# A streaming log-sum-exp on one core: in tiles 56 to 62 GpSimd folds one head of each half tile after the exp and adds no bias before it; in the prologue VectorE does the copies and one exp replaces three

## Chip, cores, metric

One core of a Trainium2 chip. The metric is the device time of one execution in microseconds. Its median before was 328.29 us (three runs, 328.19 to 328.30). Engines in the profile: PE is the tensor engine (PEld its weight loads), DVE is VectorE, ACT is ScalarE, POOL is GpSimd, SP is the sync engine, which issues the loads. SBUF is the on-chip memory that holds the tiles, PSUM the one that PE writes its sums to. In the views, the granted clock is the share of the full TensorE clock that PE was given, and the DMA share is the mean busy share of the core's 16 DMA engines, which move the data between the device's memory and SBUF.

## The reference

```python
B, S, D, H = 8, 2048, 2048, 8            # x (8, 2048, 2048) f32, bias (8, 256) f32
x_heads = x.reshape(B, S, H, D // H).transpose(0, 2, 1, 3) + bias[None, :, None, :]
x_tiled = np.repeat(x_heads, 2, axis=2)
mx  = x_tiled.max(axis=-1, keepdims=True)
lse = mx.squeeze(-1) + np.log(np.exp(x_tiled - mx).sum(axis=-1))   # (8, 8, 4096)
```

Every row of 2048 numbers is eight heads of 256. For each head: add the head's bias, exp, sum, log; each result is written twice. x is 134.2 MB and is read once.

## The kernel before

x comes in as 64 tiles of 256 rows (2.1 MB, two rows a partition, so tile halves k = 0 and k = 1) through nine buffers. From tile 56 on each half of a tile is loaded and worked on by itself; I call that a unit. There are three ways to deal with a head, and each stage (a range of tiles) deals its eight heads to them:

- "pe" heads: PE puts bias and x into PSUM, ScalarE takes exp and sums in one instruction (a head sum below);
- weighed heads: ScalarE takes exp(x) in place, VectorE multiplies by exp(bias) and sums (or, `fold`, GpSimd multiplies and halves three times to 32 columns, and VectorE adds up the rest in a small reduction);
- "g" heads: GpSimd adds the bias, ScalarE takes exp, VectorE reduces.

```python
BULK      = dict(pe=2, g0=4, late=True,  fold=0)   # heads 0-1 pe, 2-3 weighed in one piece, 4-7 g
MIXED     = dict(pe=1, g0=4, late=False, fold=0)   # head 0 pe, 1-3 weighed one by one, 4-7 g
PROMPT    = dict(pe=2, g0=8, late=False, fold=0)   # heads 0-1 pe, 2-7 weighed one by one
PROMPT_F1 = dict(pe=2, g0=8, late=False, fold=1)   # ... the last of them folded by GpSimd
PROMPT_F2 = dict(pe=2, g0=8, late=False, fold=2)   # ... the last two
STAGES = [(0, (BULK,)), (50, (MIXED,)), (56, (MIXED, MIXED)), (61, (PROMPT, PROMPT)),
          (62, (PROMPT, PROMPT_F1)), (63, (PROMPT_F2, PROMPT))]   # a pair: one mode per tile half

# prologue: bias row spread over the partitions by PE, weights exp(bias)
for i, c in enumerate(range(G0, D, MM)):
    spread(ps[i], c, c + MM)
    nc.scalar.activation(out=b_rep[:, c - G0 : c - G0 + MM], in_=ps[i], func=ACT.Copy)
for c in range(W0, W2, MM):
    w = w_ps[:, c - W0 : c - W0 + MM]
    spread(w, c, c + MM)
    nc.scalar.activation(out=w, in_=w, func=ACT.Exp)
nc.scalar.activation(out=w_sb, in_=b_rep[:, W1 - G0 :], func=ACT.Exp)

# main loop, cut to its order
for t in range(T):
    for k0, k1, c0, c1 in pieces(t):               # tile 63 comes in seven pieces of columns
        ...                                        # PE: add x to the bias in PSUM; GpSimd: g_add
        if c0 == 0 and (t < T - 1 or k0 == 0): flush(for_pool)   # the unit before: g heads, fold's sum
        done = exp_inplace(...)                    # ScalarE: exp of the weighed heads
        if hf < h1: for_pool.append(fold(...))     # GpSimd: fold
        if c0 == 0 and (t < T - 1 or k0 == 0): flush(for_pe)     # the unit before: pe heads
        for k in ...: for h in range(h0, hf): weigh(...)         # VectorE
        ...                                        # a freed buffer: load(t + NBUF)
    ...                                            # log of a finished batch; after batch 6 store()
flush(for_pe); flush(for_pool); finish_last()      # transpose, log, store of batch 7
```

The softmax here doesn't subtract the row's maximum and nothing guards it: scores larger than these inputs give would overflow.

## Time and profile before

| | before |
|---|---|
| time, us | 328.29 |
| span in the profile, us | 326.5 |
| busy: DVE, ACT, POOL, PE, us | 286.4, 278.5, 288.4, 230.7 |
| DMA rate, 50 to 260 us | 428 GB/s at a DMA share of 1.00 |
| x read | 134.2 MB |

The chain that ended last (the profile follows it back from the last instruction, at each step to what released it) closes so in the kernel before (start, duration, what):

```profile
309.90 10.19 DMA xt<-in_x_dram
...
320.12 0.63 ACT xt L257
320.75 0.01 issue
320.76 0.63 ACT xt L257
321.38 1.47 ACT xt L232 x8
```

In this profile the end hangs on the landing of a piece of tile 63 at 320.1, then on ScalarE's last exps and head sums.

### The profile page before, as it was taken

Reading aid. Unit: us, or ns where it says so; the run is one execution under the profiler, and the core shown is the slowest. Engines: PE = TensorE matmul, PEld = TensorE weight load, DVE = VectorE, ACT = ScalarE, POOL = GpSimd, SP = SyncE. Lnnn points to the kernel's source line nnn. Section 1 sums busy time; section 2 is a strip of 40 time slices with the busy share of each in tenths; the row PEclk is TensorE's granted clock in tenths of the full one; section 3 lists DMA queues with packets and bytes.
Section 4 is the critical chain, followed back from the end, with each engine's and each line's share of the span. In section 5 each row is a group of like instructions: output and inputs, shape, how many; then the busy total and the mean of one; then the engine's idle time right before and its main releaser. Section 6 shows DMA issues by size and latency. Waiting matters only on the chain.

```text
span 326.5 us, 1959 instructions
## 1 busy us (share of the span) xinstructions
PE 230.7 (71%) x391; PEld 67.5 (21%) x391; DVE 286.4 (88%) x318; ACT 278.5 (85%) x574; POOL 288.4 (88%) x88
## 2 busy tenths in 40 slices
PE   6798857777677668967798666686667355575791
PEld 2122211212122212312222212212112101222220
DVE  0029999999999999989998999989998999999994
ACT  3279999798889888799889889899888988799995
POOL 7999899979999999999998999999998999999713
PEclk9999698588967985597658778968987655555576
DMA  8999999999999999999999999999999999999993
GB/s 292 432 434 424 433 430 424 432 426 428 430 428 427 430 430 425 428 434 426 423 432 427 422 435 428 426 434 426 426 433 426 428 432 422 417 421 422 422 386 105
DMA packets 11807, 135.41 MB, mean 415 GB/s; under 512 B 1361, under 2 KB 1489, under 8 KB 2833
## 3 DMA queue, kind: packets, MB, share of 16 engines
q1 hardware_dynamic: 11696, 135.27, 98.5%
q8 instruction: 3, 0.05, 0.1%
q14 instruction: 10, 0.08, 0.1%
q0 software_dynamic: 96, 0.00, 0.0%
q10 hardware_dynamic: 2, 0.01, 0.0%
HBM read 134.23 MB, written 1.05 MB: 414 GB/s over the span
## 4 chain that ended last, share of the span: by engine, by line
DMA 69%; DVE 10%; POOL 7%; ACT 7%; PE 6%; issue 0%; SPq 0%
DMA xt<-in_x_dram 67%; DVE R L274 7%; POOL xt L251 6%; ACT xt L257 5%; PE ps L217 4%; DVE xt L267 2%; DMA b<-bparts 2%; ACT xt L232 2%; PE ps L202 1%; DMA brow<-in_bias_dram 0%; POOL brest L165 0%; POOL brest L167 0%; POOL b L170 0%; PE tpair L330 0%; POOL bparts L164 0%
## 5 line engine op out<-in xcount | busy, mean ns | idle before, releaser
L251 POOL TENSOR_TENSOR xt<-xt,b_rep 128x2048 f32<-128x2048 f32 (+1 forms) x66 | 277.5, 4209 | 22.1 <-DMA xt<-in_x_dram 21.9
L217 PE MATMUL ps<-xt,ident 128*128 128x512 f32 (+1 forms) x244 | 175.7, 852 | 78.8 <-DMA xt<-in_x_dram 78.5
L257 ACT ACTIVATE xt<-xt 128x3072 f32<-128x3072 f32 (+3 forms) x91 | 185.7, 2062 | 20.2 <-POOL xt L251 19.3
L274 DVE TENSOR_REDUCE R<-xt 128x12 f32<-128x3072 f32 (+1 forms) x56 | 181.4, 3240 | 2.3 <-ACT xt L257 0.6
L232 ACT ACTIVATE xt<-ps 128x256 f32<-128x256 f32 x234 | 86.8, 394 | 11.2 <-PE ps L217 11.1
L267 DVE TENSOR_TENSOR xt<-xt,w_ps 128x1024 f32<-128x1024 f32 x50 | 60.9, 1218 | 32.7 <-ACT xt L257 32.6
L217 PEld LDWEIGHTS ps<-xt,ident 128*128 128x128 f32 x244 | 55.3, 256 | 152.8 <-DMA xt<-in_x_dram 111.2
L232 ACT ACTIVATION_READ_ACCUMULATOR xt<-ps 128x1 f32 x234 | 51.0, 220 | 0.0
L202 PE MATMUL ps<-b,ones 3*128 3x512 bf16 (+1 forms) x122 | 47.5, 457 | 2.8 <-ACT xt L232 1.6
L285 DVE CUSTOM_DVE_ANT_0 xt<-xt,w_ps 128x256 f32<-128x256 f32 x95 | 34.0, 417 | 0.3 <-ACT xt L257 0.3
L202 PEld LDWEIGHTS <-ones 3*128 3x128 bf16 x122 | 8.0, 97 | 82.1 <-issue 82.1
L274 DVE TENSOR_REDUCE R_last<-xt 128x4 f32<-128x1024 f32 x10 | 12.2, 1218 | 0.0
L301 POOL TENSOR_TENSOR xt<-xt,w_sb 128x256 f32<-128x256 f32 (+1 forms) x2 | 2.1, 1032 | 8.7 <-ACT xt L257 8.5
L340 ACT ACTIVATE res<-tpair 64x512 f32<-64x512 f32 x7 | 4.1, 588 | 3.5 <-PE tpair L330 3.4
L174 PE MATMUL w_ps<-brow,ones 1*128 1x512 f32 x6 | 6.0, 1109 | 1.3 <-ACT w_ps L186 1.3
L330 PE MATMUL tpair<-ident,R 128*64 128x128 f32 x14 | 3.8, 364 | 3.7 <-DVE R L274 3.7
L186 ACT ACTIVATE w_ps<-w_ps 128x512 f32<-128x512 f32 x3 | 1.7, 582 | 5.4 <-PE w_ps L174 5.4
L174 PE MATMUL ps<-brow,ones 1*128 1x512 f32 x4 | 3.7, 1089 | 2.5 <-DMA brow<-in_bias_dram 2.5
L285 DVE DVE_READ_ACCUMULATOR2_ANT R_last<- 128x1 f32 x63 | 5.3, 84 | 0.0
L180 ACT ACTIVATE b_rep<-ps 128x512 f32<-128x512 f32 x2 | 1.2, 597 | 3.6 <-PE ps L174 3.6
L285 DVE DVE_READ_ACCUMULATOR2_ANT R<- 128x1 f32 x36 | 3.0, 85 | 0.0
L351 PE MATMUL tpair<-ident,R_last 128*128 128x128 f32 x1 | 0.5, 477 | 3.6 <-ACT xt L232 3.6
(24 smaller groups left out, 18.0 us busy)
## 6 DMA issues: line engine op xcount, KB each, us to landing
xt<-in_x_dram SPq DMA_DIRECT2D x56, 2048.0 KB, 31.9
xt<-in_x_dram SPq DMA_DIRECT2D x14, 1024.0 KB, 21.0
xt<-in_x_dram SPq DMA_DIRECT2D x5, 256.0 KB, 11.3
out_dram<-res SPq DMA_DIRECT2D x1, 896.0 KB, 8.0
xt<-in_x_dram SPq DMA_DIRECT2D x2, 384.0 KB, 16.5
out_dram<-res_last SPq DMA_DIRECT2D x1, 128.0 KB, 1.7
b<-bparts POOLq DMA_DIRECT2D x3, 1.0 KB, 6.0
brow<-in_bias_dram ACTq DMA_DIRECT2D x1, 8.0 KB
```

Source lines behind the costliest of these rows:

```text
L174: nc.tensor.matmul(dst, lhsT=ones, rhs=brow[:, c0:c1], start=True, stop=True)
L202: nc.tensor.matmul(p, lhsT=ones3, rhs=each_row(b3, 0, n, kb - ka), start=True, stop=False,)
L217: mm = nc.tensor.matmul(p, lhsT=ident, rhs=xts[t % NBUF][:, ka:kb, 0:n], start=False, stop=True,)
L232: act = nc.scalar.activation(out=xts[t % NBUF][:, k, c : c + Dh], in_=p[:, c : c + Dh], func=ACT.Exp, accum_out=sums[:, k, h : h + 1],)
L251: add = nc.gpsimd.tensor_tensor(out=v, in0=v, in1=each_row(b_rep, c - G0, D - c, k1 - k0), op=ALU.add)
L257: return on_x(t, nc.scalar.activation(out=v, in_=v, func=ACT.Exp), [after])
L267: mul = nc.vector.tensor_tensor(out=f, in0=f, in1=each_row(w_ps, h0 * Dh - W0, n, k1 - k0), op=ALU.mult,)
L274: red = nc.vector.tensor_reduce(out=sums[:, k0:k1, h0:H], in_=v.rearrange("p k (h j) -> p k h j", j=Dh), op=ALU.add, axis=mybir.AxisListTy ...
L285: ttr = nc.vector.tensor_tensor_reduce(out=v, in0=v, in1=w, scale=1.0, scalar=0.0, op0=ALU.mult, op1=ALU.add, accum_out=dst,)
L301: done = nc.gpsimd.tensor_tensor(out=v, in0=v, in1=w_sb[:, h0 * Dh - W1 : h1 * Dh - W1], op=ALU.mult)
L330: nc.tensor.transpose(out=tp[0:nr, k], in_=R[b][:, k].rearrange("p h n -> p (h n)"), identity=ident,)
L340: nc.scalar.activation(out=res[:, b], in_=tv, func=ACT.Ln)
```

## The change

Intent: from tile 56 on no head goes through GpSimd's slow bias add ahead of the exp; one head is folded by GpSimd instead, after the exp, and one summed by ScalarE. In the prologue the idle VectorE does the copies, and one exp in place of three breaks ScalarE's and PE's turn-taking.

```diff
+SINGLE_F1 = dict(pe=1, g0=8, late=False, fold=1)
 STAGES = [
     (0, (BULK,)),
     (50, (MIXED,)),
-    (56, (MIXED, MIXED)),
-    (61, (PROMPT, PROMPT)),
-    (62, (PROMPT, PROMPT_F1)),
+    (56, (SINGLE_F1, SINGLE_F1)),
+    (62, (PROMPT_F1, SINGLE_F1)),
     (63, (PROMPT_F2, PROMPT)),
 ]
@@ prologue
-        nc.scalar.activation(
-            out=b_rep[:, c - G0 : c - G0 + MM], in_=ps[i], func=ACT.Copy
-        )
+        nc.vector.tensor_copy(b_rep[:, c - G0 : c - G0 + MM], ps[i])
     for c in range(W0, W2, MM):
-        w = w_ps[:, c - W0 : c - W0 + MM]
-        spread(w, c, c + MM)
-        nc.scalar.activation(out=w, in_=w, func=ACT.Exp)
+        spread(w_ps[:, c - W0 : c - W0 + MM], c, c + MM)
+    nc.scalar.activation(out=w_ps, in_=w_ps, func=ACT.Exp)
```

## The prediction

> **What bounds the kernel now.** I read the page's slices first, then the chain that ended last, the sync engine's waits, the stretches of the last microseconds, and the timeline of ScalarE and VectorE there. From the page of the kernel before (one digit or figure per 8.16 us):
>
> ```profile
> DVE  0029999999999999989998999989998999999994
> DMA  8999999999999999999999999999999999999993
> GB/s 292 432 434 424 433 430 424 432 426 428 430 428 427 430 430 425 428 434 426 423 432 427 422 435 428 426 434 426 426 433 426 428 432 422 417 421 422 422 386 105
> ```
>
> Three compute engines are 85% to 88% busy, which tempts one to look for the gain there. But the DMA row is full from the second slice to the last but one. 134.2 MB of x have to come in; at the 428 GB/s that the stretch from 50 to 260 us shows, that is 134.2 / 0.428 = 313.6 us of the 326.5 us span. The rest is about 2 us before the first bytes, some slow transfer near the end, and the tail after the last landing.
>
> Could the transfers have been late because a buffer came free late? The sync engine's waits (what it waited for, us in total, times, longest):
>
> ```profile
> SPq L135 <- DVE R L274: 230.1, 50, 18.1
> SPq L135 <- DMA xt<-in_x_dram: 51.5, 19, 4.5
> SPq L344 <- DMA xt<-in_x_dram: 2.1, 1, 2.1
> ```
>
> The loads do wait for VectorE's reductions, but the page gives 31.9 us from issue to landing of a 2048 KB load, and one such load takes 2.097 / 0.428 = 4.9 us of transfer. So some 6.5 loads are in the queue when a new one joins; freeing a buffer a microsecond earlier makes a request stand in line longer, and lands nothing earlier. The first nine loads alone are 9 x 4.9 = 44 us of transfer, while VectorE's first reduction starts at 23.9 us.
>
> The end, by stretches (us, then PE, PEld, DVE, ACT, POOL busy with counts, granted clock, DMA share, GB/s):
>
> ```profile
> 260.00:310.00 50.00, 31.61 (x51) 9.79 (x51) 49.43 (x149) 44.68 (x75) 46.13 (x16) 0.50 1.01 423
> 310.00:316.00 6.00, 5.92 (x10) 1.50 (x9) 6.00 (x34) 5.72 (x12) 0.00 (x0) 0.64 1.01 396
> 316.00:321.00 5.00, 2.85 (x7) 0.73 (x6) 4.57 (x26) 4.68 (x14) 4.03 (x7) 1.00 0.98 298
> ```
>
> and the timeline of ScalarE in the tail (start, duration, what, idle before and who ended it):
>
> ```profile
> 317.70 2.11 ACT L257 ACTIVATE xt<-xt 128x768 f32<-128x768 f32 x3
> 320.12 1.27 ACT L257 ACTIVATE xt<-xt 128x512 f32<-128x512 f32 x2 [0.31 <-DMA xt<-in_x_dram]
> 321.29 0.36 ACT L232 ACTIVATE xt<-ps 128x256 f32<-128x256 f32 x1
> ...
> 322.36 0.39 ACT L232 ACTIVATE xt<-ps 128x256 f32<-128x256 f32 x1
> 322.62 0.22 ACT L232 ACTIVATION_READ_ACCUMULATOR xt<-ps 128x1 f32 x1
> 323.41 0.38 ACT L357 ACTIVATE res_last<-tpair 128x256 f32<-128x256 f32 x1 [0.57 <-PE tpair L351]
> ```
>
> ScalarE had caught up and stood idle for 0.31 us until a piece of tile 63 landed at about 320.1. From there: two exps (1.27), four head sums (1.4), transpose, logarithm, store: 6.4 us to the end. VectorE runs beside that and begins its last reduction at 322.40, ending with ScalarE within 0.3 us. So the end is last landing plus a tail of tile 63.
>
> **What the Trainium skill says.** "Perfetto Trace Analysis", Roofline, says that one core alone may exceed its HBM share but is bounded by its 16 DMA engines at about 435 GB/s. The trace agrees: 423 to 430 GB/s at a DMA share of 1.0. "ScalarE: Activation LUTs", What ACT_TABLE_LOAD costs, gives an ACTIVATE with immediate scale and bias as 186 ns + 0.833 ns per element, consecutive ones overlapping by 93 ns. Here 768 elements took 0.834 us and 1536 took 1.473 us: agreement (0.826, 1.466). "GPSIMD Engine Reference", Specifications, says GpSimd contends with VectorE instructions that have two SBUF inputs. VectorE's weighing took 418 ns with weights in PSUM and 422 ns with weights in SBUF, so at this size little shows either way; under the new plan heads 1 to 6 have their weights in PSUM, and only GpSimd reads the SBUF weights in stages 56 to 61.
>
> **Prologue.** Two PSUM-to-SBUF copies (0.60 us each on ScalarE) go to an idle VectorE. Three exps of 512 (0.58 each), each made to alternate with a pair of matmuls (about 2.1 us), become one of 1536, about 1.47. Before: ScalarE's preparation ends at 14.55. After: ten fp32 matmuls back to back from 2.46, about 9.5 us, so 12; plus 1.5 and 0.5: near 14. Worth 0.5 us to ScalarE at most, and nothing waits for it: the first x matmul waits for the three bias rows that GpSimd writes with a DMA landing at 14.25, unchanged, and ScalarE's first head sum is at 17.44. The first load is issued at 0.74 either way. Value at the end: 0.
>
> **Last eight tiles.** Tiles 56 and up are already loaded in half tiles, and the pieces of tile 63 do not change, so the list of transfers is identical. What changes is work per half tile (1.05 MB, 2.48 us apart by the waits of PE):
> - GpSimd: 2.36 us of bias add (128x1024) go; a fold of one head comes in: 0.79 + 1.19 + gaps, 316.44 to 318.50 = 2.06 in the present trace (tile 62).
> - ScalarE: exps of 768 and 1024 (0.83 + 1.05 - overlap) become one of 1792: 186 + 0.833 x 1792 = 1.68. With a head sum, from a pace of 2.04 to about 1.95.
> - VectorE: 3 weighings and a 1024 reduction, pace 2.155 (288.85 to 310.40 for ten units), become 6 weighings at a pace of 0.342 and a small reduction of about 0.11: 2.165.
> - PE: half the bias and x columns in tile 61 and in half of 62. It waits for data; no gain.
> All three remain under 2.48.
>
> The tightest is VectorE, which enters the stage late. In the trace before it starts tile 56 at 288.85, though that half tile landed near 282.6, because tile 55 comes through GpSimd's add first. With no idle, afterwards: first unit 2.05, eleven at 2.165 = 23.8, tile 62's halves 1.82 (5 weighings) and 2.165, one small reduction 0.11: 288.85 + 29.95 = 318.8 when it is ready for tile 63. Before, it was ready at 318.64, having idled 0.17 for GpSimd. So +0.16; the 0.26 us that it then idled for ScalarE at 319.3 absorb that. ScalarE at tile 62: +0.2 (1792 for 1536) and -0.36 (one head sum fewer): ready about 0.1 earlier for a piece that lands at 320.1 anyway. GpSimd is at its last two folds at the same time as before. Sum: 0 + 0 + 0, within 0.2 us.
>
> **Rivals.** (1) The small reduction sits in VectorE's order between two units and waits for GpSimd's fold: 2.06 us of fold against 2.05 of weighing, a tie. While VectorE runs behind, the fold is long done. Should each unit lose 0.2 us to that wait, the backlog of 6 us at tile 56 would not drain, and 13 x 0.2 = 2.6 us would show in the tail: 330.5. For it: no slack; against it: the one such wait in the trace lost 0.17 us and was when VectorE had caught up. (2) The relieved engines speed up DMA: 423 GB/s at 260 to 310 against 428. If engine traffic were the cause, 25 us x 1.2% = 0.3 us would come back: 328.0. But bulk stages have as busy a GpSimd at 428, and the half tiles have shorter rows; more likely the rows. (3) The prologue brings the whole pipeline forward by 0.5 to 2 us: 326.5 to 327.8. Against: DMA is at full share from 4 us on, and the first landing does not move.
>
> **Range and chances.** Point 328.2, hardly moved from 328.29: the transfer floor and tail are unchanged, rival 2 pulls slightly one way and rival 1 the other. The repeats of before lie within 0.11 us, so the range is for the rivals: 327.3 (2 and some of 3) to 329.3 (a third of 1). 2% is 6.6 us: more than the tail holds to win, and more than rival 1 would lose. Faster 0.01, same 0.98, slower 0.01.
>
> **What would show it.** DMA share full and last x landing near 320; ScalarE idle for a DMA just before its last two 512 exps; VectorE's last reduction within 0.3 us of 322.4; GpSimd's busy time down by some 10 x (2.36 - 2.0) = 4 us, without effect on the span. I am wrong if VectorE's idle time in 289 to 316 names GpSimd with more than 1 us, if its last reduction passes 323, or if the last landing moves by more than half a microsecond; then a change on a compute engine reached the queue in a way that I do not see.

## The result

328.17 us (four runs, 328.05 to 328.69) against 328.24 us for the kernel before (four runs, 328.19 to 328.30): ratio 1.0001, 95% interval 0.9984 to 1.0018. No difference. Ratios here and below are the mean time of one kernel's fast runs over that of the other's of the same rounds, so not quite the ratio of the medians quoted.

The page's slices of the kernel after:

```profile
DVE  2029999999999999999999999989998999999995
DMA  7999999999999999999999999999999999999993
GB/s 290 430 436 428 429 430 422 434 426 424 432 430 423 434 425 424 434 428 424 433 426 423 433 430 424 432 430 424 434 427 426 432 428 422 420 418 421 423 382 114
```

Slice by slice the transfers are within 11 GB/s of those of before. Stretches of the end (length, then busy time of PE, PEld, DVE, ACT, POOL, granted clock, DMA share, GB/s):

```profile
260.00:310.00 50.00, 30.57 (x51) 9.96 (x52) 49.41 (x207) 44.18 (x66) 40.93 (x48) 0.50 1.01 422
310.00:316.00 6.00, 4.82 (x8) 1.50 (x8) 6.00 (x38) 4.58 (x7) 4.32 (x11) 0.50 1.02 397
316.00:321.00 5.00, 5.00 (x7) 1.20 (x6) 4.52 (x27) 5.00 (x13) 3.81 (x7) 0.50 0.99 301
```

GpSimd's work went down from 46.13 to 40.93 us in the first of them and up from 0 to 4.32 in the second; rates went nowhere (423, 396 and 298 GB/s before). In the third, ScalarE is now busy without a break, and the clock that PE was granted is 0.50 where it was 1.00. The chain that ended last has another shape:

```profile
294.92 20.18 DMA xt<-in_x_dram
...
315.12 1.71 ACT xt L254
316.82 0.02 issue
316.85 0.42 DVE xt L282
...
322.22 0.34 DVE xt L282
322.57 0.14 DVE R_last L312
```

It leaves the transfers at 315.1, with the landing of the second half of tile 62, and then runs through VectorE (16 weighings, two small reductions), not through a landing of tile 63. ScalarE had no idle time between 315.12 and its last head sum at 322.38. The end is the same to 0.1 us: the last transpose starts at 322.85, before at 322.89.

The trace also holds the landing records of each load, 16 to a load, as many as there are DMA engines; the views don't print them, the packed trace has them. What uses a load waits for the last of the 16: in before, 15 of the piece that ScalarE waited for had landed by 318.74 and the last at 320.09, and the exp began at 320.12. The last piece of tile 63 was complete at 320.73 in before and at 320.19 in after.

### The profile page after: what moved, and what is told of

Same layout as the page of the kernel before. It is cut to its first block, busy times and chain, and to the rows that moved or that the text cites. A ratio compares the mean times of both kernels' runs of the same rounds, so it can differ in the third digit from the quotient of the medians.

```text
span 326.4 us, 2048 instructions
## 1 busy us (share of the span) xinstructions
PE 236.1 (72%) x391; PEld 69.1 (21%) x391; DVE 288.0 (88%) x383; ACT 275.4 (84%) x554; POOL 287.6 (88%) x130
## 4 chain that ended last, share of the span: by engine, by line
DMA 74%; DVE 9%; POOL 9%; ACT 6%; PE 2%; issue 0%; SPq 0%; DVEq 0%
DMA xt<-in_x_dram 71%; POOL xt L248 7%; ACT xt L254 5%; DVE R L271 5%; DMA b<-bparts 2%; DVE xt L264 2%; DVE xt L282 2%; PE ps L214 1%; DMA brow<-in_bias_dram 0%; ACT xt L229 0%; POOL brest L167 0%; POOL brest L165 0%; POOL b L170 0%; PE ps L199 0%; POOL bparts L164 0%
## 5 line engine op out<-in xcount | busy, mean ns | idle before, releaser
L248 POOL TENSOR_TENSOR xt<-xt,b_rep 128x2048 f32<-128x2048 f32 x56 | 254.2, 4539 | 22.1 <-DMA xt<-in_x_dram 22.1
L214 PE MATMUL ps<-xt,ident 128*128 128x512 f32 (+1 forms) x244 | 180.2, 873 | 76.6 <-DMA xt<-in_x_dram 76.1
L254 ACT ACTIVATE xt<-xt 128x3072 f32<-128x3072 f32 (+4 forms) x81 | 185.4, 2304 | 19.7 <-POOL xt L248 16.7
L199 PE MATMUL ps<-b,ones 3*128 3x512 bf16 (+1 forms) x122 | 49.0, 469 | 4.8 <-DMA b<-bparts 2.9
L282 DVE CUSTOM_DVE_ANT_0 xt<-xt,w_ps 128x256 f32<-128x256 f32 x128 | 45.2, 412 | 0.5 <-ACT xt L254 0.5
L306 POOL TENSOR_TENSOR xt<-xt 128x128 f32<-128x128 f32 (+3 forms) x45 | 15.9, 353 | 3.5
L298 POOL TENSOR_TENSOR xt<-xt,w_sb 128x256 f32<-128x256 f32 (+1 forms) x15 | 11.5, 765 | 6.7 <-ACT xt L254 6.6
L183 ACT ACTIVATE w_ps<-w_ps 128x1536 f32<-128x1536 f32 x1 | 1.4, 1435 | 9.4 <-PE w_ps L174 9.4
L282 DVE DVE_READ_ACCUMULATOR2_ANT R_last<- 128x1 f32 x93 | 7.2, 78 | 0.0
L312 DVE TENSOR_REDUCE R_last<-xt 128x1 f32<-128x32 f32 (+1 forms) x15 | 2.7, 179 | 0.0
```

The costliest lines, as they stand in the source:

```text
L199: nc.tensor.matmul(p, lhsT=ones3, rhs=each_row(b3, 0, n, kb - ka), start=True, stop=False,)
L214: mm = nc.tensor.matmul(p, lhsT=ident, rhs=xts[t % NBUF][:, ka:kb, 0:n], start=False, stop=True,)
L248: add = nc.gpsimd.tensor_tensor(out=v, in0=v, in1=each_row(b_rep, c - G0, D - c, k1 - k0), op=ALU.add)
L254: return on_x(t, nc.scalar.activation(out=v, in_=v, func=ACT.Exp), [after])
L282: ttr = nc.vector.tensor_tensor_reduce(out=v, in0=v, in1=w, scale=1.0, scalar=0.0, op0=ALU.mult, op1=ALU.add, accum_out=dst,)
L298: done = nc.gpsimd.tensor_tensor(out=v, in0=v, in1=w_sb[:, h0 * Dh - W1 : h1 * Dh - W1], op=ALU.mult)
```

## The experiments

All ran beside the kernel before on one chip for each group; the kernel before had medians of 328.26, 328.37 and 328.34 in the three groups. Every run was fast (no run of a kernel over 1.5% above its fastest), or a single run.

### One part at a time

`e1_prologue_only` has the new prologue and the old stages; `e2_stages_only` the reverse. Their edits are the two halves of the diff above.

> The kernel before with only the new prologue. Transfer theory (the x transfers run at full share from 4 us on and fix the end): ScalarE is ready about 1.2 us earlier (13.34 for 14.55, as in the trace of after), the first x matmul still waits for the bias rows near 14.2, time 328.2 within 0.3. Rival, the prologue sets when the pipeline starts: 327.0 or less.

Measured: 328.34 us, ratio 1.0000 (0.9985 to 1.0015). ScalarE's preparation ended at 14.3 in this run, whose first matmuls came 0.9 us later than in after; the single exp took 1.44 us. The end of this run matters for what follows: it has the old stages, yet ScalarE's last five exps run without the wait that before shows among them. First after, then this run:

```profile
317.79 3.13 ACT L254 ACTIVATE xt<-xt 128x768 f32<-128x768 f32 x5
318.08 3.14 ACT L254 ACTIVATE xt<-xt 128x768 f32<-128x768 f32 x5
```

VectorE ends last here as well (its last reduction starts at 322.79). The last piece of tile 63 was complete at 320.41, 0.32 us sooner than in before.

> The kernel before with only the new stages for tiles 56 to 63. Transfer theory: 328.2 within 0.3, and the tail as in after: VectorE's last reduction starts near 322.5 and ends after ScalarE's last head sum. Rival, the two parts cancel (prologue wins what the stages lose, or the reverse): this one and the prologue alone would differ from before by over 0.5 us in opposite directions.

Measured: 328.26 us, ratio 0.9995 (0.9980 to 1.0009). VectorE's last reduction started at 322.34, behind ScalarE, as in after. So the two parts do not cancel: each is worth nothing that these runs can resolve (0.2%).

### How much slack the start has

```diff
     nc.scalar.activation(out=w_sb, in_=b_rep[:, W1 - G0 :], func=ACT.Exp)
+    nc.vector.memset(res, 0.0)
+    idle = res.rearrange("q b p k r -> q (b p k r)")
+    for _ in range(4):        # e4_delay10: 10
+        nc.scalar.activation(out=idle, in_=idle, func=ACT.Copy)
```

> After, with four copies of 3584 elements (about 3.1 us each, 12.3 in all) put into ScalarE's prologue. ScalarE's first head sum moves from 17.3 to about 25.6, VectorE's first work from 22.5 to about 31. Transfer theory: the first freed buffer (27.1 in after) comes at about 35, still 9 us before the nine loads in the queue are through (44 to 46), so the time stays 328.2 within 0.4. Rival, a late start of the engines is paid in full: 336.

Measured: 328.25 us, ratio 0.9996 (0.9980 to 1.0013). The copies took 12.84 us, ScalarE's first head sum came at 26.93, 9.6 us later than in after, and VectorE's first work at 31.15 for 22.51. Nothing of it reached the end. A prologue that can lose nine microseconds for nothing cannot gain by winning one.

> After, with ten such copies (30.8 us): ScalarE's first head sum at about 44, VectorE's first work at about 49.5, first freed buffer at about 54, after the queue has run dry near 46. Transfer theory: now the delay shows, as a hole of about 8 to 10 us in the transfers, and VectorE, which has only some 12 us of idle between 22.5 and the end, limits the catching up: 338 to 341. Rival, paid in full: 355.

Measured: 339.48 us, ratio 1.0339 (1.0323 to 1.0354). VectorE began at 49.67 and had no wait after that. The stretches of this run, in the columns used above, show the queue running dry:

```profile
44.00:46.00 2.00, 0.00 (x0) 0.00 (x0) 0.00 (x0) 2.00 (x4) 2.00 (x1) 0.50 0.98 418
46.00:48.00 2.00, 1.55 (x3) 0.56 (x3) 0.00 (x0) 2.00 (x7) 1.62 (x2) 0.50 0.25 107
48.00:50.00 2.00, 2.00 (x3) 0.71 (x3) 0.33 (x1) 2.00 (x4) 2.00 (x1) 0.50 0.00 0
...
52.00:54.00 2.00, 1.69 (x4) 0.47 (x3) 2.00 (x1) 2.00 (x4) 0.25 (x1) 1.00 0.00 0
54.00:56.00 2.00, 1.15 (x3) 0.39 (x3) 1.97 (x3) 2.00 (x8) 0.00 (x0) 1.00 0.60 119
```

The nine loads were through at about 46.5 and the first freed buffer came after 54: some eight microseconds of silence. The two runs bracket how much later VectorE may start at no cost: over 8 us (31.15 for 22.51), under 28 (49.67).

### Fewer bytes, the same instructions

```diff
+    def cut(t, c1):
+        return 7 * Dh if NBUF <= t < 50 else c1
-                    out=xts[t % NBUF][:, k0:k1, c0:c1],
-                    in_=rows_of(t)[:, k0:k1, c0:c1],
+                    out=xts[t % NBUF][:, k0:k1, c0:cut(t, c1)],
+                    in_=rows_of(t)[:, k0:k1, c0:cut(t, c1)],
@@ exp_inplace
-        return on_x(t, nc.scalar.activation(out=v, in_=v, func=ACT.Exp), [after])
+        sc = 0.0 if NBUF <= t < 50 else 1.0
+        return on_x(t, nc.scalar.activation(out=v, in_=v, func=ACT.Exp, scale=sc), [after])
```

> After, with an eighth of each row not loaded for tiles 9 to 49 (10.7 MB less; wrong results on purpose, the exps there take a scale of 0 to stay finite), every compute instruction kept at its size. Transfer theory: 10.7 / 0.428 = 25 us less transfer, but VectorE has 288 us of work after 22.5 and idles only some 12 us, so the time falls by about 12 us, to 314 to 318, and VectorE is then the bound. Rival, the engines or their waits already set the time: within 1 us of 328.

Measured: 313.64 us in one run, wrong results as meant. That is 14.7 us under the kernel before, a little more than forecast (just below the 314 to 318): with every instruction queued, VectorE's are run one into the next, and its busy time is 284.4 us for 288.0. The page's chain by engine:

```profile
DVE 91%; DMA 3%; PE 2%; POOL 2%; ACT 1%; issue 1%; DVEq 0%
```

Take bytes away and the kernel gets faster until VectorE is the bound, from its first work to its last. So transfer bounds the kernel, and VectorE stands under 15 us behind it.

### What sets the tail

The chain of after contradicted what I had written about the end, so I tried to move the landing. The 0.9 MB store of batches 0 to 6 was issued at about 315, while tile 63's loads were on their way; here it is held back:

```diff
                 if hf < h1:
+                    if t == T - 1:
+                        nc.gpsimd.tensor_copy(res[:, B - 2, 0], res[:, B - 2, 0])
+                        store()
                     for_pool.append(fold(t, k0, hf, h1, sums, done))
@@ end of the loop over tiles
-            if fb == B - 2:
-                store()
```

> After, with the 0.9 MB store of batches 0 to 6 held back (by a small GpSimd copy into its source ahead of tile 63's fold) until about 319, so that it no longer shares the DMA engines with tile 63's loads. What I wrote in the prediction, that the end is the last landing plus a tail of tile 63: the landing comes 1.5 to 2 us earlier, and the time with it, 326.4 or so. The theory from the trace of after, that from the landing of tile 62's second half (315.1) on VectorE has 17 instructions without a break and ScalarE is as full: landing earlier, time unchanged, 328.2 within 0.3.

Measured: 328.89 us, ratio 1.0016 (1.0002 to 1.0030). Stretches, first of after, then of this run:

```profile
317.00:318.00 1.00, 1.00 (x2) 0.32 (x2) 1.00 (x7) 1.00 (x7) 0.92 (x2) 0.50 1.04 321
318.00:319.00 1.00, 1.00 (x3) 0.10 (x1) 1.00 (x7) 1.00 (x2) 0.84 (x4) 0.50 0.99 291
319.00:320.00 1.00, 1.00 (x2) 0.50 (x2) 1.00 (x6) 1.00 (x3) 1.00 (x1) 0.50 1.02 287
```

```profile
317.00:318.00 1.00, 1.00 (x2) 0.50 (x2) 0.86 (x5) 1.00 (x7) 0.73 (x2) 0.50 0.44 170
318.00:319.00 1.00, 1.00 (x2) 0.00 (x0) 1.00 (x7) 1.00 (x4) 0.84 (x3) 0.50 0.21 82
319.00:320.00 1.00, 1.00 (x3) 0.44 (x3) 1.00 (x6) 1.00 (x2) 1.00 (x3) 0.50 0.12 45
```

The time is above both forecasts. And the run did not do what it was built for. The rates fall from 317 on because the store's bytes are gone from them, but the landing of tile 63 did not come sooner: of the last piece 14 of the 16 shares had landed by 318.96 (318.87 in after), the other two at 320.28 and 320.47 (319.91 and 320.19). The DMA share of 0.12 between 319 and 320 fits that: about 2 of 16 engines still at work. The whole tail is 0.3 us later: the second half of tile 62 landed at 315.4 (315.1 in after), VectorE's last reduction came at 322.78 (322.49). So whether an earlier landing of tile 63 would buy anything is not tested by this run. It gives no sign that the store keeps tile 63's last piece back. The rest of the small loss has a place: the held store was issued at 319.3, landed 6.6 us later, moved only some 205 GB/s, and the last store, behind it, took 2.2 us to land for 1.7. "SBUF — State Buffer", Door 1, says that partitions 0 to 63 reach only 8 of 16 DMA ports, about 218 GB/s; the store reads 64 partitions, and the 205 GB/s of this run, at a DMA share of 0.95, agree; no run varies the partitions.

### What a wait for the fold would have looked like

```diff
+SINGLE_F2 = dict(pe=1, g0=8, late=False, fold=2)
-    (56, (SINGLE_F1, SINGLE_F1)),
+    (56, (SINGLE_F2, SINGLE_F2)),
```

> After, with two heads instead of one folded by GpSimd in tiles 56 to 61 (and five instead of six weighed by VectorE). This is what rival 1 would have looked like: 1.28 + 1.66 + gaps = about 3.0 us per half tile on GpSimd against 2.48 between arrivals. Twelve units from 288.2 end at 324.2, then 2.0 + 2.0 + 3.0 of folds for tiles 62 and 63: VectorE's last reduction at about 331, time 335 to 337, VectorE's idle put down to GpSimd. If the relief of VectorE mattered more: 328 or less.

Measured: 337.47 us in one run, 0.5 above the forecast's range. VectorE's waits in this run (engine, what it wanted, for whom, us in total, times, longest) hold the line

```profile
DVE R_last L313 <- POOL xt L307: 12.2, 12, 1.1
```

twelve waits of about 1 us. GpSimd's folds follow each other at 2.97 us, 0.5 more than an arrival. In after VectorE's list has no such line at all: there the folds follow each other at 1.95 us.

### Relieving the tail

If VectorE's run from tile 62's second half sets the end, a weighing fewer there should show.

```diff
-    (62, (PROMPT_F1, SINGLE_F1)),
+    (62, (SINGLE_F1, PROMPT_F1)),
@@ main loop, ahead of the exp
+            if t == T - 2 and k0 == 1:
+                flush(for_pe)
```

> After, with the head fewer for VectorE moved to tile 62's second half (which lands last) and ScalarE's head sum of tile 62's first half put ahead of the exp of the second, into the 0.73 us in which ScalarE waits for that landing. Theory, VectorE's unbroken run from the landing of tile 62's second half to the end sets the tail in after: one weighing of 0.34 fewer on it, and ScalarE's exp 0.21 shorter; VectorE's last reduction at 322.1 for 322.5, ScalarE done near 322, time 327.8. Rival, the last landing sets it: 328.2. The difference is near the spread of the repeats (0.2 us), so the trace decides more than the time.

Measured: 328.70 us, ratio 1.0013 (1.0000 to 1.0025): no gain, and the time is above both forecasts. Its chain shows what ended last:

```profile
315.29 2.08 PE ps L214 x2
317.37 0.54 PE ps L199
317.90 2.01 PE ps L214 x2
319.91 0.53 PE ps L199
320.44 2.02 PE ps L214 x2
322.46 0.02 issue
322.49 0.85 ACT xt L229 x4
```

With two pe heads in tile 62's second half, PE has three wide units in a row, each 2.54 us at the granted clock of 0.50, and ends at 322.46; ScalarE waits 0.49 us for it. VectorE too lost what it had won, 0.57 us of waits for GpSimd and ScalarE. I had left PE out. So this run does not test whether VectorE's run ends the tail of after.

`e9_tail_store` is the same with the store held back to 316.9 only (the GpSimd copy ahead of tile 62's second fold).

> The same, with the 0.9 MB store held back only until about 316.5, so that it begins when the x loads are nearly through and is done near 322 to 323, ahead of the last small store. If the late store cost 0.6 us in the run with the store at 319 because the last store queued behind it, that loss goes: equal to the run with the tail's order alone, 327.8 within 0.2; VectorE's last reduction where it is there, since an earlier landing of tile 63 gives it nothing. If a landing earlier does help once VectorE is relieved: 327.3 or less.

Measured: 328.47 us, ratio 1.0006 (0.9992 to 1.0019). This too is above both forecasts. PE ends the tail here as well (its last wide unit was over at 322.7), and again the last piece of tile 63 was complete no sooner (320.62, against 320.37 in `e8_tail_order`). Whether an earlier landing would turn into time stays open, with and without PE's chain. No version beat the kernel before.

## Why the prediction was right

The time, 328.17 us, is within 0.1 of the point. Step by step:

- **Transfer bounds the kernel.** Shown: fewer bytes at equal instructions took 14.7 us off (e5, one run); ScalarE delayed by nearly 10 us gave none (e3); only a delay beyond the queue's 46 us gave a hole (e4).
- **Prologue worth 0.** Shown by e1, and by e3's slack. ScalarE was ready at 13.3 in after; I had said near 14.
- **Three paces under 2.48 us.** In after VectorE's was 2.14 (forecast 2.165), ScalarE's 1.94 (1.95), GpSimd's 1.95 (2.06). Right.
- **VectorE ready for tile 63 at 318.8.** It was at 319.02. But the sum assumed no idle time; VectorE had drained its backlog and stood 0.48 us for tile 62's second exp, so the near hit is partly luck.
- **Rival 1, waits for the fold.** No such wait in after (the forecast for it has a slip: 2.6 us on top of 328.2 is 330.8, not 330.5); e7 shows how it looks when the fold is slower than the arrivals, 12.2 us of waits and 9 us of time.
- **Rival 2, DMA relieved by a quieter GpSimd.** 422 GB/s for 423 between 260 and 310: no.
- **VectorE's weighing against GpSimd.** I took 418 ns with weights in PSUM and 422 ns in SBUF to show little contention. The four weighings with weights in SBUF began at 312.12, 314.17, 316.23 and 322.06, and in that stretch GpSimd worked only from 316.44 to 321.64: the two hardly met, so the comparison shows nothing of contention. Little hung on it, as in tiles 56 to 61 of the new plan VectorE weighs with weights in PSUM alone.
- **"The end is last landing plus a tail of tile 63."** It fits the one profile of before that I read, not after, and the sign I named, ScalarE idle for a DMA before its last two 512 exps, did not appear: it ran five exps from 317.79 to 320.92 without a break. Nor does it hold for the old stages as such: in e1, which has them, it did not appear either. What differs is when the last piece was complete: 320.73 in before, 320.41 in e1, 320.19 in after, 320.06 in e2. In after the last two exps began 0.22 and 0.11 us after their pieces had landed, so it took a tenth of a microsecond more for the wait to come back. By the trace, after ends with work that piled up behind tile 62's second half: VectorE has no idle time from 316.85 to its end. No run moved the landing of tile 63 by itself, so this is read from the chain and not shown by an experiment. The time stayed, as far as the traces show, because ScalarE's end in before (322.8) and VectorE's end in after (322.7) are close; PE gets as late with one more wide unit (e8).
- **"I am wrong if the last landing moves by more than half a microsecond."** It moved by 0.54 us, to the earlier side, so by its letter this sign came. Single traces don't settle whether the change did it: e1, with the old stages, lies between (0.32 us earlier than before). The other two signs of being wrong did not come: VectorE's list names no wait for GpSimd, and its last reduction began at 322.49.
- **GpSimd's busy time down by 4 us.** It went from 288.4 to 287.6. I counted ten units' folds; there are 13 more folds than before, about 1.75 us busy each, 22.7 us, against 23.3 of adds saved.

Open: why the last of the 16 shares of tile 63's last piece lands 1.1 to 1.8 us behind the fourteenth (before, after and six of the runs); and why PE was granted 1.00 in the tail of before and 0.50 in after, with less for PE to do. The last goes with the stages and not with the prologue (between 316 and 321 us: 0.98 in e1, 0.51 in e2), but no run shows the cause.

## What to carry to other kernels

When loads stand some six deep in a full queue, ask of a change whether it moves the first issue, the bytes, or the work after the last landings; anything else is slack, and a deliberate delay measures that slack in one run. In the tail do not stop at the last landing: add up each engine's work behind the last two or three units, all engines, at the clock that the trace shows there. Where the engines end close together (in after VectorE at 322.7, ScalarE at 322.4, PE's last wide unit at 321.4), moving work off one can hand the end to another, as in e8. And check that an experiment did what it was built for by the event that it was to move: a rate that falls (e6) need not mean that anything landed sooner.

## What the Trainium skill lacked or had wrong

- "GPSIMD Engine Reference", Performance versus the Vector engine: gives 4497 ns for a two-input add of 2048 elements and about 2.6 cycles an element, but nothing for small ones, which decide a fold. Here 2048, 1024, 512 and 256 elements took 4.54, 2.36, 1.27 and 0.73 us: about 0.2 us fixed plus 2.1 ns an element (worked out from these).
- "ScalarE: Activation LUTs", What ACT_TABLE_LOAD costs: its formula held for plain exps, but no figure is given for the accumulator output. Here a separate read of 0.19 to 0.23 us follows in the tail, and 256-element head sums from PSUM run at 0.36 us, where the formula would give 0.31.
- "VectorE: DVE Perf Modes" has no duration for a multiply with sum: 256 elements took 0.42 us, at a pace of 0.34.
